# Hybrid decoder step on one core: the attention's output stores are issued by ScalarE instead of SP

## The chip, the cores and the metric

One NeuronCore of a Trainium2 chip runs the whole program in a single launch. The metric is device time in microseconds (us) of that launch. Engines are named as in the profile: PE is TensorE's matmuls and PEld its weight loads, DVE is VectorE, ACT is ScalarE, POOL is GpSimd, and SP is SyncE, which in this kernel issues nearly all DMAs. "SPq" and "ACTq" are the sequencers of those engines.

## The reference

One inference step of a decoder with a recurrent layer and an attention layer, for two groups of tokens:

```python
x = x + rms_norm(recurrent_mixer(rms_norm(x)))          # RG-LRU layer
k, v, logf = shared_kv(x)                               # K, V, log-forget, new rows
# attention layer, 16 heads of 64, queries q and gate g from x @ w_in:
s = q @ k^T * 64**-0.5 + cq[query] - ck[key]            # cq, ck: running sums of logf
s = where(k_pos <= q_pos, s, -inf)
o = softmax(s) @ v
x = x + rms_norm((o * silu(g)) @ w_out)
```

The first group is a new sequence ("prompt") of 2048 tokens of width 1024. The second is 8 sequences of 8 new tokens ("sample") that each attend over 4096 older keys and values, which lie in 32 pages of 128 rows each, found through a page table. All is float32; matmul operands are split into a high and a low part where that precision is wanted.

## The kernel before

The program goes through the recurrent layer in two chunks of tokens and through the projections to K, V, Q and the gate in three. Then comes the attention of the prompt, and last the output projection. The attention over the old pages ("decode") is a Python generator that is drawn on beside these: its work is dealt out into the projections and the prompt's attention by a table of costs. A scheduler of the framework then sets the final order on each engine from its own timeline; the two versions are scheduled separately, so instructions can change places well away from an edit.

**Prompt attention.** It consists of 64 *units*, one for each of 16 heads (`h`) and each quarter of 512 queries (`qc`). A unit goes through 4 to 16 key tiles of 128; over all units that is 640 ticks. Each tick is: a score tile `st` on PE (L1651 and L1652, and L1654 where the causal mask cuts), its exponential on ACT (L1662), a running sum on POOL (L111), and, two to eight ticks later in groups, the product with V on PE (`ops`, L1675). The score tiles have two PSUM banks while the decode runs. The maxima that the exponentials need come from a second pass of scores on PE (`sx`, L1438), which DVE reduces (L1440, L1444).

**The end of a unit.** `finish` (from L1465) books two steps with `later`, a list of functions due some ticks ahead. `copies` runs two ticks after the last product: ACT copies the unit's output from PSUM into a 64x512 tile `oT` (L1478, two copies; the profile calls that buffer `attw`, since it is a lent piece of one). `store` runs two ticks after that: SP writes `oT` to the DRAM tensor `og_d` (L1483; `ogd` in the profile). The buffers of `oT` serve four units in turn. `project` reads `og_d` back at the very end (L1732).

**Decode.** For each sequence and half of the heads ("turn"), SP loads 8 groups of four K pages (L1144) and 8 of four V pages (L1146) into four buffers `raw` of four pages each. DVE transposes the K pages (`ktr`, L1218), PE makes scores (`dS`, L1202), ACT exponentiates (L1256), PE multiplies with V pages straight from `raw` (`dO`, L1290).

**The order on SP.** SP takes its instructions strictly in order: page loads, loads of queries and keys (L1405 to L1421), stores. The helper `paged()` puts what is recorded inside it behind the newest page group on SP:

```python
    def paged():
        return tc.issue_after(place["S"]) if "S" in place else ExitStack()
```

**Completion semaphores.** The framework gives the DMAs that SP issues eight completion semaphores in turn (`DMAHW0` to `DMAHW7`). Each DMA first waits until the DMA before it on its semaphore has landed, so at most eight are under way, and the ninth waits for the first.

Of the kernel before, what the change touches and what calls it, by code (L numbers as in the profile page):

```python
# [28 lines left out]
HD = 64  # L29
# [61 lines left out]
def tile_hawk_fox(  # L91
# [8 lines left out]
    V, A, G, T, S = nc.vector, nc.scalar, nc.gpsimd, nc.tensor, nc.sync  # L100
# [19 lines left out]
    def paged():  # L120

        return tc.issue_after(place["S"]) if "S" in place else ExitStack()
# [49 lines left out]
    def dt_(name, shape):  # L172
        return dram.tile(shape, F32, name=name, tag=name)
# [6 lines left out]
    og_d = [dt_(f"ogd{qc}", [D, 512]) for qc in range(SEQ // 512)]  # L180
# [197 lines left out]
    later = Later()  # L378
# [985 lines left out]
    def attention(es):  # L1364
# [100 lines left out]
        def finish(u, ops, acc):  # L1465
            h, qc = units[u]
            pr, h2 = divmod(h, 2)
            if u % 8 == 0:
                oTs_["sums"] = rings["sums"]()
            sums = oTs_["sums"]  # L1470
            if u % 2 == 0:
                oTs_["o"] = rings["oT"]()
            oT = oTs_["o"][u % 2 * HD:(u % 2 + 1) * HD, :]

            def copies():
                view = oT.rearrange("d (a r c) -> d a r c", a=2, r=2)
                for r in range(2):
                    A.copy(view[:, :, r, :], ops[r * HD:(r + 1) * HD, :].rearrange("d (a c) -> d a c", a=2))  # L1478
                later.after(2, store)

            def store():
                with paged():
                    S.dma_start(og_d[qc][h * HD:(h + 1) * HD, :], oT)  # L1483

            later.after(2, copies)
            accs.append((qc, acc))
            if len(accs) == 4 or h == H - 1:
                later.after(2, lambda todo=accs[:]: total(h2, sums, todo, h >= H - 2))
                accs.clear()
            if u >= len(units) - 4:  # L1490
                later.after(5, lambda: norm(pr, sums, qc, 1))
            elif u % 8 == 7:
                later.after(5, lambda: norm(pr, sums, 0, 4))

        def total(h2, sums, todo, single):


            ps = maxima("tot")
            for qc, acc in todo:
                T.matmul(ps[qc * 32:(qc + 1) * 32, :], ones[:, :32], acc[:, :], start=True, stop=True)  # L1500
            cs = todo[-1][1]
            rows = slice(0, P) if len(todo) == 4 else slice(qc * 32, (qc + 1) * 32)
            A.copy(cs[rows, :], ps[rows, :])
            if single:
                for qc, acc in todo:
                    j = qc * 2 + h2
                    S.dma_start(sums[j * 16:(j + 1) * 16, :], cs[qc * 32:qc * 32 + 1, :].rearrange("o (r c) -> o r c", r=16))
            else:
                S.dma_start(sums[h2 * HD:(h2 + 1) * HD, :], cs[:, :].rearrange("(q z) (r c) -> z q r c", z=32, r=16)[0])

        def norm(pr, sums, q0, n):

            ps_ = slice(q0 * 32, (q0 + n) * 32)
            V.reciprocal(sums[ps_, :], sums[ps_, :])
            V.tensor_copy(rs[0][ps_, :], sums[ps_, :])
            tt(V, rs[1][ps_, :], sums[ps_, :], f(rs[0][ps_, :]), ALU.subtract)
            for x in range(2):
                if n == 4:
                    for z in range(2):
                        S.dma_start(r_d[:, x, z, pr, :].rearrange("q (r c) -> q r c", r=16),  # L1520
                                    f(rs[x][z * HD:(z + 1) * HD, :]))
                else:
                    S.dma_start(r_d[q0, x, :, pr, :].rearrange("z (r c) -> z r c", r=16), f(rs[x][ps_, :]))
# [119 lines left out]
        for u, (h, qc) in enumerate(units):  # L1643
            for k in range(nks[u]):
# [21 lines left out]
                def product(u=u, h=h, todo=pair, early=group == 8, acc=acc, last=(k == nks[u] - 1)):  # L1666


                    nonlocal ops
                    if todo[0][0] == 0:  # L1670
                        ops = ops2[:, u % 2 * 256:u % 2 * 256 + 256]

                    def mm(k, lo, p, r):
                        a0 = (lo // P + 1 - r) // 2
                        return T.matmul(ops[r * HD:(r + 1) * HD, a0 * P:], vvs[h % 2][:, k, :],  # L1675
                                        p[:, :].rearrange("p (a r c) -> p a r c", a=2, r=2)[:, a0:, r, :],
                                        start=(k == 0), stop=(last and k == todo[-1][0] - 1 + r))

                    together([partial(mm, k, lo, p, r) for k, lo, p, _ in todo for r in range(2) if lo <= (2 + r) * P],
                             [todo[-1][3]])  # L1680
                    for k, lo, p, _ in todo:
                        if k and not early:
                            tt(a_l(), acc[:, lo:], acc[:, lo:], p[:, lo:], ALU.add)
                    if last:
                        finish(u, ops, acc)
# [329 lines left out]
```

## Time and profile before

| | |
|---|---|
| time, 3 runs | 2919.55, 2931.59 (median), 2937.87 us |
| the profiled execution | 2919.81 us, span 2918.1 us |
| PE busy over the span | 2747.1 us (94%) |
| ACT busy over the span | 1267.6 us (43%) |
| granted PE clock | 0.978 of full speed |
| HBM traffic | 222 GB/s over the span |

The profile is of one execution. "Idle before, releaser" is time in which an engine stood still, and the instruction whose semaphore ended that. An engine's `DMA_DIRECT2D` row is the time that its sequencer takes to issue a DMA; the transfer itself runs on the 16 DMA engines afterwards.

### The profile page before, as it was taken

How to read it: one execution, taken by the hardware profiler on the slowest of the kernel's cores; microseconds unless marked ns; L12 is line 12 of the kernel's file. 1: busy time of each engine (PE TensorE's matmuls, PEld its weight loads, DVE VectorE, ACT ScalarE, POOL GpSimd, SP SyncE). 2: the span in 40 equal slices, each digit the busy share in tenths (PEclk: the TensorE clock that was granted, in tenths of full speed). 3: DMA queues.
4: the chain of work that ended last, by engine and by line, in shares of the span. 5: the costliest groups of instructions: out<-in, count | busy, mean ns of one | idle time of the engine just before them, and what ended most of it. 6: DMA issues, size and time to landing. Idle time of an engine off the chain costs nothing.

```text
span 2918.1 us, 59421 instructions
## 1 busy us (share of the span) xinstructions
PE 2747.1 (94%) x21086; PEld 2224.8 (76%) x21086; DVE 1828.1 (63%) x3971; ACT 1267.6 (43%) x2874; POOL 1098.0 (38%) x1207
## 2 busy tenths in 40 slices
PE   5998999999998999999999999999999999999998
PEld 5997789988898997887888766565666665666787
DVE  7877457244256775676565676767677766655465
ACT  4656342222234665533334345444444544455221
POOL 1654110000003652100001265756565655659554
PEclk9999999999999999999999999999999999999999
DMA  4224536789745536689999978778788777862454
GB/s 127 80 86 125 169 124 188 203 243 300 224 142 177 178 107 191 215 303 325 341 314 333 338 261 293 239 255 277 253 271 269 255 259 240 284 222 61 131 184 131
DMA packets 484789, 636.03 MB, mean 218 GB/s; under 512 B 100888, under 2 KB 293145, under 8 KB 477276
## 3 DMA queue, kind: packets, MB, share of 16 engines
q1 hardware_dynamic: 484204, 630.13, 66.6%
q8 instruction: 167, 2.74, 0.4%
q0 software_dynamic: 288, 2.10, 0.3%
q14 instruction: 130, 1.06, 0.1%
HBM read 512.78 MB, written 133.85 MB: 222 GB/s over the span
## 4 chain that ended last, share of the span: by engine, by line
PE 55%; DMA 9%; DVE 7%; ACT 4%; SPq 3%; issue 2%; POOL 1%; DVEq 0%; ACTq 0%; POOLq 0%
PE ops L1675 8%; PE st L1651 5%; PE sx L1438 4%; PE st L1652 4%; PE dS L1202 3%; PE dO L1290 3%; PE y L389 3%; PE y L387 3%; PE y L388 3%; DMA raw<-in_cache_k_dram 2%; PE kv L387 2%; PE kv L389 2%; PE kv L388 2%; PE qg L387 2%; PE qg L389 2%
## 5 line engine op out<-in xcount | busy, mean ns | idle before, releaser
L1218 DVE STREAM_TRANSPOSE ktr<-raw 128x1024 f32<-128x1024 f32 x256 | 308.0, 1225 | 97.6 <-DMA raw<-in_cache_k_dram 73.5
L1440 DVE TENSOR_REDUCE mxs<-sx 128x1 f32<-128x512 f32 x384 | 253.8, 680 | 157.6 <-PE sx L1438 156.8
L387 PE MATMUL kv<-wh,xh 128*128 128x256 f32 (+3 forms) x1088 | 307.7, 287 | 3.0 <-ACT wh L432 1.7
L389 PE MATMUL kv<-wh,xl 128*128 128x256 f32 (+3 forms) x1088 | 307.1, 284 | 0.4 <-DMA xl<-xld 0.4
L388 PE MATMUL kv<-wl,xh 128*128 128x256 f32 (+3 forms) x1088 | 306.6, 284 | 0.4 <-DVE wl L433 0.3
L433 DVE SCALAR_TENSOR_TENSOR wl<-wst,gv,wh 128x256 fp32r<-128x256 f32 (+1 forms) x384 | 171.1, 494 | 130.7 <-ACT wh L432 130.6
L432 ACT ACTIVATE wh<-wst,gv 128x256 fp32r<-128x256 f32 (+1 forms) x384 | 164.4, 499 | 200.4 <-DMA wst<-in_b_w_in_dram 83.0
L389 PE MATMUL qg<-xh,wl 128*128 128x384 f32 (+2 forms) x640 | 227.5, 357 | 2.2 <-DVE wl L433 2.2
L387 PE MATMUL qg<-xh,wh 128*128 128x512 f32 (+2 forms) x640 | 229.2, 359 | 0.0
L388 PE MATMUL qg<-xl,wh 128*128 128x512 f32 (+2 forms) x640 | 228.1, 358 | 0.0
L387 PEld LDWEIGHTS kv<-wh,xh 128*128 128x128 f32 (+1 forms) x1088 | 201.1, 186 | 8.7 <-issue 3.7
L389 PEld LDWEIGHTS kv<-wh,xl 128*128 128x128 f32 (+1 forms) x1088 | 202.3, 186 | 3.1 <-issue 2.4
L388 PEld LDWEIGHTS kv<-wl,xh 128*128 128x128 f32 (+1 forms) x1088 | 201.5, 186 | 4.1 <-issue 2.5
L1166 POOL TENSOR_TENSOR qw<-qb,amask 128x128 f32<-128x128 f32 x64 | 26.7, 422 | 459.9 <-PE dS L1202 197.7
L1662 ACT ACTIVATE attl<-st 128x512 f32<-128x512 f32 (+3 forms) x236 | 120.5, 524 | 129.2 <-PE st L1652 61.4
L1444 DVE CUSTOM_DVE_ANT_0 sx<-sx,maskb 128x128 f32<-128x128 f32 (+3 forms) x256 | 123.1, 488 | 70.9 <-PE sx L1438 64.9
L1662 ACT ACTIVATE attw<-st 128x512 f32<-128x512 f32 (+3 forms) x224 | 118.0, 550 | 102.4 <-PE st L1652 68.1
L1290 PE MATMUL dO<-raw,sc 128*32 128x256 f32 x2048 | 141.9, 398 | 20.7 <-DMA raw<-in_cache_v_dram 19.9
L111 POOL TENSOR_TENSOR atth<-atth,attl 128x512 f32<-128x512 f32 (+3 forms) x119 | 128.1, 1079 | 65.9 <-ACT attl L1662 47.7
L111 POOL TENSOR_TENSOR atth<-atth,attw 128x512 f32<-128x512 f32 (+3 forms) x116 | 132.3, 1141 | 38.9 <-ACT attw L1662 22.1
L1202 PE MATMUL dS<-ktr,qw 128*32 128x128 f32 x4096 | 129.8, 282 | 14.4 <-DVE ktr L1218 13.5
L925 ACT COPY kf<-kv 128x256 f32<-128x256 f32 (+1 forms) x136 | 49.0, 366 | 217.1 <-PE kv L389 152.7
(359 smaller groups left out, 7651.8 us busy)
## 6 DMA issues: line engine op xcount, KB each, us to landing
raw<-in_cache_k_dram SPq DMA_DIRECT2D x512, 256.0 KB
raw<-in_cache_v_dram SPq DMA_DIRECT2D x512, 256.0 KB
wst<-in_w_kv_dram SPq DMA_DIRECT2D x48, 512.0 KB
wst<-in_b_w_in_dram SPq DMA_DIRECT2D x48, 512.0 KB
xt<-in_x_prompt_dram SPq DMA_DIRECT2D x32, 512.0 KB
wst<-in_a_w_in_dram SPq DMA_DIRECT2D x64, 256.0 KB
out_dram<-kf SPq DMA_DIRECT2D x128, 128.0 KB
cb<-cd SPq DMA_DIRECT2D x14, 1024.0 KB
```

What stands on the lines that cost most here:

```text
L111: eng.tensor_tensor(out, a, b, op=op)
L387: T.matmul(ps, lh(k), rh(k), start=(k == 0), stop=False)
L388: T.matmul(ps, lh(k), rl(k), start=False, stop=False)
L389: end = T.matmul(ps, ll(k), rh(k), start=False, stop=(k == nk - 1))
L432: A.activation(wh[:, k, :], st[:, k, :], AF.Copy, scale=gk)
L433: V.scalar_tensor_tensor(wl[:, k, :], st[:, k, :], gk, f(wh[:, k, :]), op0=ALU.mult, op1=ALU.subtract)
L1202: return T.matmul(sp[c * 32:(c + 1) * 32, h * P:(h + 1) * P], qw[:, pp * 2 + h // 2, h % 2 * 2 + x, :], kt[:, :, :, i0:i0 + 8], start=(x = ...
L1218: behind("V", V.transpose(t.kts[pp][:, n], raw[:, :, pp * 256:(pp + 1) * 256]).ins)
L1290: return T.matmul(op[c:c + 32, :256], t.sc[:, i // 4, m, a * 4:(a + 1) * 4, :].rearrange("p h q -> p (h q)"), raw[:, m, a * 256:(a + 1) * ...
L1440: r = V.reduce_max(mx[:, j, ck:ck + 1], ps[:, :w], axis=AX.X)
L1662: pair.append((k, lo, p, A.activation(p[:, lo:], ps[:, lo:], AF.Exp)))
L1675: return T.matmul(ops[r * HD:(r + 1) * HD, a0 * P:], vvs[h % 2][:, k, :], p[:, :].rearrange("p (a r c) -> p a r c", a=2, r=2)[:, a0:, r, : ...
```

## The change

The function `store` goes. ACT issues the store itself, in `copies`, right behind its two copies:

```diff
                 for r in range(2):
                     A.copy(view[:, :, r, :], ops[r * HD:(r + 1) * HD, :].rearrange("d (a c) -> d a c", a=2))
-                later.after(2, store)
-
-            def store():
-                with paged():
-                    S.dma_start(og_d[qc][h * HD:(h + 1) * HD, :], oT)
+                A.dma_start(og_d[qc][h * HD:(h + 1) * HD, :], oT)
 
             later.after(2, copies)
```

64 DMAs of 128 KB move from SP's queue to ACT's. Lines behind the edit have numbers lower by four in the changed kernel (L1662 becomes L1658). Nothing else is written differently.

The first place is on SP, around the store of the second unit (`ogd_73`); the words in brackets are the semaphores that an instruction waits for: a DMA's own completion semaphore and those of engines. `TENSOR_LOAD` and `ISA` fetch page numbers. Before:

```order
L1144 DMA raw<-in_cache_k_dram 128x512 [waits DMAHW5_49]
L1421 DMA qa_17881<-qd 128x512 [waits DMAHW6_49]
L1415 DMA qbt_17880<-qd 64x512 [waits DMAHW7_49,PE_49]
L1483 DMA ogd_73<-attw 64x512 [waits DMAHW0_49,Activation_49]
L1136 TENSOR_LOAD pt_130
L1146 ISA
L1146 DMA raw<-in_cache_v_dram 32x4x512 [waits DMAHW1_49,PE_49]
```

and with the change:

```order
L1144 DMA raw<-in_cache_k_dram 128x512 [waits DMAHW5_49]
L1421 DMA qa_17881<-qd 128x512 [waits DMAHW6_49]
L1415 DMA qbt_17880<-qd 64x512 [waits DMAHW7_49,PE_49]
L1136 TENSOR_LOAD pt_130
L1146 ISA
L1146 DMA raw<-in_cache_v_dram 32x4x512 [waits DMAHW1_49,PE_49]
```

The store is gone from between the query load and the V page; the V page keeps its semaphore, number 1, and so number 0 is still passed over for the store.

The second place is on ACT, around the copies of the same unit. Before:

```order
L1478 COPY attw<-ops 64x2x128 [waits PE_49]
L1478 COPY attw<-ops 64x2x128
L1459 ACTIVATE qbt_17877<-mps,st_p 4x128 [waits PE_49,Pool_49]
L1459 ACTIVATE qbt_17877<-mps,st_p 4x128 x3
L1662 ACTIVATE atth_19402<-st 128x512 [waits PE_49,Pool_49]
```

and with the change:

```order
L1478 COPY attw<-ops 64x2x128 [waits PE_49]
L1478 COPY attw<-ops 64x2x128
L1459 ACTIVATE qbt_17877<-mps,st_p 4x128 [waits PE_49,Pool_49]
L1459 ACTIVATE qbt_17877<-mps,st_p 4x128 x3
L1479 DMA ogd_73<-attw 64x512 [waits DMAHW0_49,Activation_49]
L1658 ACTIVATE atth_19402<-st 128x512 [waits PE_49,Pool_49]
```

The store now stands on ACT ahead of the next exponential, and it brings both of its waits with it: for ACT's own copies, and for `DMAHW0`, whose DMA before it is one that SP issues.

## Prediction

> **What bounds the kernel now.** I read the page's head first, then the busy times by stage, then the waits of the stage in which the stores lie.
>
> ```profile
> span 2918.1 us, 59421 instructions
> core 0: us, PE busy (x) PEld busy (x) DVE busy (x) ACT busy (x) POOL busy (x), PEclk, DMA share, GB/s
> 0.00:1670.00 1670.00, 1563.40 (x11355) 1428.65 (x11355) 1012.51 (x2258) 724.50 (x1555) 347.93 (x519) 0.98 0.66 209
> 1670.00:2640.00 970.00, 916.75 (x8469) 593.72 (x8467) 659.54 (x1352) 461.95 (x1141) 590.86 (x568) 0.97 0.78 259
> 2640.00:2725.00 85.00, 82.71 (x476) 53.81 (x477) 36.02 (x83) 42.93 (x100) 68.31 (x62) 0.96 0.16 43
> ```
>
> The rows are stretches of the span. The prompt's attention runs from 1670 to about 2725 us, up to 2640 with the transfers busy (DMA share 0.78) and then without them (0.16). The stores lie there and nowhere else; up to the first of them the order on all engines is the same in both versions, so the first 1670 us stay. PE is busy 916.75 + 82.71 = 999.5 of 1055 us: it is the bound, and only its 55.5 idle us can be won. What PE waits for there:
>
> ```profile
> PE dO L1290 <- DMA raw<-in_cache_v_dram: 13.5, 6, 3.4
> PE sx L1438 <- DVE mxs L1440: 7.5, 13, 1.5
> PE st L1651 <- ACT attl L1662: 7.3, 16, 1.5
> PE sx L1438 <- DVE mxs L1444: 5.0, 4, 2.3
> PE st L1651 <- ACT attw L1662: 4.3, 12, 1.5
> PE dS L1202 <- DVE ktr L1218: 2.5, 1, 2.5
> PEld dO L1290 <- DMA raw<-in_cache_v_dram: 6.3, 8, 2.8
> ```
>
> Each row gives total us, times, longest. Late pages cost PE 13.5 us and its weight loads 6.3 (partly the same moments), late K transposes 2.5, late exponentials 7.3 + 4.3.
>
> **What the change takes from SP.**
>
> ```profile
> SPq L1483 <- ACT attw L1478: 55.9, 22, 7.5
> SPq L1483 <- ACT attw L1478: 37.4, 18, 5.5
> SPq L1483 <- ACT attw L1478: 18.5, 4, 7.5
> SPq L1146 <- DVE ktr L1218: 14.2, 4, 7.0
> SPq L1146 <- PE dO L1290: 12.8, 3, 6.9
> L1483 SPq DMA_DIRECT2D ogd<-attw x64: 463/521/1447, 1678.0 to 2722.3; - x64
> ```
>
> The first three rows are SP's wait at the store for ACT's copies: in the whole attention, before 2640, and after. 37.4 us of it hold up page loads. The last row gives the issue of one store (minimum, median, maximum): 64 x 0.521 = 33 us that also leave SP. How much of this reaches PE? Never more than late pages cost: 13.5 + 6.3 + 2.5 = 22.3 us, and the rows of L1146 say that a page load that comes earlier often meets a buffer that is still in use (14.2 + 12.8 us). Of PE's long waits for V pages, the loads just ahead show this:
>
> ```profile
> 1847.79 1.98 SPq L1144 DMA_DIRECT2D raw<-in_cache_k_dram  x4
> 1857.76 3.13 SPq L1146 DMA_DIRECT2D raw<-in_cache_v_dram  x4
> 1864.34 1.83 PE L1290 MATMUL dO<-raw,sc 128*32 128x256 f32 x16 [2.07 <-DMA raw<-in_cache_v_dram]
> 2339.02 0.54 SPq L1483 DMA_DIRECT2D ogd<-attw  x1
> 2339.75 0.60 SPq L1146 DMA_DIRECT2D raw<-in_cache_v_dram  x1
> ```
>
> At 1864 us the V pages were late because their loads stood still until 1857.76 behind no store. At 2339 a store stood in a burst of page loads and put the next one off by 2339.75 - 2339.02 = 0.73 us. I take one or two such slots, 0.7 to 1.4 us, for each of PE's six waits, 4 to 8 us, and put the gain at **5 us** (ends 0 and 22). The 18.5 us after 2640 I put at nothing: no page follows there, and PE is busy 82.71 of 85 us.
>
> **What it puts on ACT: the issue.** No DMA is issued by ACT in this trace. The nearest row is SP's 0.521 us above; the ends are nothing and 64 x 0.521 = 33 us. What covers it is ACT's own idle time in front of its exponentials:
>
> ```profile
>   PE st L1652: 181.6, 170
>   PE st L1654: 123.5, 114
>   PEld st L1651: 60.3, 141
>   PE st L1651: 14.1, 37
> ```
>
> Of 640 exponentials 170 + 114 = 284 begin after ACT waited for PE, 305.1 / 284 = 1.07 us each; the rest follow without a pause. The last two rows are the other side: 141 of PE's 640 score tiles already wait for an exponential, since with two banks tile k+2 needs the exponential of tile k. So 22% of delays on ACT hit PE at once (7 us of 33), and at most the 56% that meet no pause (18 us). I take **9 us**, near the lower, because that one is counted at PE itself.
>
> The Trainium skill ("Perfetto Trace Analysis", DMA Instruction — HWDGE) says that such an interval ends when the sequencer "is now free for the next instruction". By it ACT is blocked for the whole 0.52 us, as assumed; if the issue instead ran beside the next exponential, the term would be 0. No row here shows ACT issuing.
>
> **What it puts on ACT: a wait for SP's transfers.** This is the term that decides. The store must find its completion semaphore free, and the DMA before it there is one of SP's, eight issues earlier. SP, which comes by in its own order, finds that mostly over; ACT comes when its copies are done. The unit whose order was shown:
>
> ```profile
> 1689.30 0.59 SPq L1405 DMA_DIRECT2D atth<-kd  x1
> ...
> 1695.04 0.58 SPq L1415 DMA_DIRECT2D qbt<-qd  x1
> 1697.56 0.52 SPq L1483 DMA_DIRECT2D ogd<-attw  x1
> 1691.70 0.74 ACT L1478 COPY attw<-ops 64x256 f32<-64x256 f32 x2 [3.34 <-PE ops L1675]
> 1692.47 1.11 ACT L1459 ACTIVATE qbt<-mps,st_p 4x128 fp32r<-4x128 f32 x4
> 1694.33 0.60 ACT L1662 ACTIVATE atth<-st 128x512 f32<-128x512 f32 x1 [0.76 <-PE st L1652]
> 2720.38 0.74 ACT L1478 COPY attw<-ops 64x256 f32<-64x256 f32 x2
> 2722.25 0.58 SPq L1483 DMA_DIRECT2D ogd<-attw  x1
> ```
>
> The copies end at 1691.70 + 0.74 = 1692.44; the store goes out only at 1697.56, 5.1 us later, though SP had nothing to issue from 1695.62 on: the key load L1405 of 1689.30 (1 MB) is its predecessor on the semaphore. On ACT the store will be reached at 1692.47 + 1.11 = 1693.58 and keep the exponential of 1694.33 waiting until about 1697.5. Between that unit and the last one (2721.12 to 2722.25, 1.1 us) 35 of the 64 stores go out more than 0.25 us after their copies, 88 us in sum. 88 us is the upper end of ACT's wait, since in this execution every predecessor had landed by the time of the store, and 0 the lower, if SP pulls ahead enough.
>
> Where between? In a burst SP issues thus, and transfers take so long:
>
> ```profile
> 1967.39 3.55 SPq L1146 DMA_DIRECT2D raw<-in_cache_v_dram  x4
> 2339.75 5.91 DMA raw<-in_cache_v_dram
> 2508.61 3.03 DMA raw<-in_cache_v_dram
> ```
>
> Eight issues take 0.65 to 0.9 us each, 5 to 7 us; the transfers on the chain of waits take 3 to 6. At SP's own place the predecessor is done for some 1.1 us on average, so of each lateness I strike 1.1 us: 52 us are left, in 27 units. Half of the stores stand behind one more exponential (0.6 us), which takes 8 off: **44 us in about 19 waits**. Since SP no longer stops for ACT, it will run ahead of where it was; I strike a third, 29 us. ACT's pauses swallow up to 1 us of each wait, and what is left of the 29 is about 17: **17 us** of late score tiles on PE.
>
> **The sum.** -5 (pages) + 9 (issue) + 17 (waits) = +21. A PE that comes later finds other inputs ready: of its 13.5 + 7.5 + 5.0 + 2.5 = 28.5 us for pages and DVE I let a third, 9 us, go under. That leaves **+12 us**: 2919.8 + 12 = 2932 on the scale of the profiled execution, which ran 11.8 us under the median; on the median, 2931.6 + 12 = **2943 us**. The two schedules also differ in many small swaps on PE and DVE, which the trace can't price; they stand on either side.
>
> **The rivals.**
>
> *ACT's waits pass through whole* (ends slower). SP doesn't pull ahead: it is held by buffers (L1146 above), and each stop of ACT makes PE release those buffers later, so SP stays as late as now. ACT then waits near 88 us in 35 places, less 1 us of pause each is 53, plus 9 for issues, less 5 and 9: +48, **2980 us**. It decides from a mean wait of 2 us at the 64 stores. For it: the lateness is seen. Against it: in 22 units SP was early, and gains 37.4 us.
>
> *SP's freedom wins* (ends faster). SP's 37.4 us move every later page ahead, the predecessors land before ACT comes, and the issues sit in ACT's pauses. Then only the gain is left, 5 to 22 us: about -12, **2920 us**. For it: DMA share 0.78, so transfers have room. Against it: PE's waits for pages mostly follow other causes.
>
> *The change does little either way.* The two waits cancel and only SP's issue time is saved, which lies beside PE's work: -4 to +4, **2931 us**. The Trainium skill ("DMA: Bandwidth & Descriptors", Issuing engines are not separate DMA queues) states this case: all issuers share the 16 DMA engines, and issuing from several "will only save the time on the sequencer". The trace agrees that SP has 33 us of such time; the rule leaves out that the new issuer can stop.
>
> **How the numbers follow.** My forecast 0.43, waits passing whole 0.22, SP's freedom 0.20, little either way 0.15. The range takes in the forecast, the gain down to its end (2931.6 - 22 = 2910) and the rival's time with half its spread: 2908 to 2982; left out are 0.10 above and 0.07 below. A measurement of this kernel tells about 1% (29 us) from no change. Faster by more needs more than every page wait gone: 0.08. Slower by more is the first rival and a tail of the forecast: 0.25. Within: 0.67.
>
> **What would show it.** Right: waits of ACT at L1479 or behind it for DMAs, 20 to 45 us in 15 to 25 places; waits of PE for exponentials grown from 14 to some 30 us; no wait of SP for L1478; waits for V pages a little under 13.5; attention (first store to last) 5 to 25 us longer. Wrong: if ACT's waits are under 10 us, SP did pull ahead; if the store's issue on ACT is far from 0.52 us, that term goes; if stages before 1670 us differ, it is not this change.

## The result, and the profile after

| | before | after |
|---|---|---|
| time, 5 runs each (median, lowest to highest) | 2928.39 us (2919.55 to 2937.87) | 2954.63 us (2948.39 to 2956.55) |
| the profiled execution | 2919.81 us, span 2918.1 us | 2951.92 us, span 2950.2 us |
| granted PE clock of the profiled execution | 0.978 | 0.973 |

The changed kernel takes 1.0105 times as long, with a 95% interval of 1.0082 to 1.0128: 26 us more by the medians. The forecast was 12 us more. A second measurement, told below, gave 1.0095 (1.006 to 1.013).

The stages of the changed kernel, as the first rows of the prediction show them for the kernel before (stretch in us, its length, then the busy time of each engine, the granted PE clock, the DMA share and GB/s):

```profile
span 2950.2 us, 59327 instructions
core 0: us, PE busy (x) PEld busy (x) DVE busy (x) ACT busy (x) POOL busy (x), PEclk, DMA share, GB/s
0.00:1670.00 1670.00, 1560.28 (x11352) 1423.47 (x11353) 1010.50 (x2256) 724.36 (x1555) 348.70 (x520) 0.99 0.66 209
1670.00:2640.00 970.00, 900.15 (x8272) 578.34 (x8272) 633.24 (x1316) 439.73 (x1098) 563.61 (x547) 0.95 0.76 251
2640.00:2757.00 117.00, 111.91 (x679) 72.17 (x676) 62.55 (x126) 65.01 (x143) 93.75 (x82) 0.98 0.33 102
```

Up to 1670 us nothing moved. The first exponential of the attention ends at 1670.6 us before and at 1670.7 us after, the stretch behind the last one takes 213.0 and 213.1 us. From the first to the last of the 640 exponentials it is 1034.5 us before and 1066.5 us after: all 32 us of the profiled pair are in the attention, and "in the attention" below means from the first to the last of these exponentials. Two numbers of the second row against the row of before carry the rest. PE is busy 900 us of 970 instead of 917, and its granted clock there is 0.95 instead of 0.97.

PE's waits by what ended them (total us, times, longest), of after:

```profile
PE dO L1290 <- DMA raw<-in_cache_v_dram: 16.6, 7, 7.2
PE st L1647 <- ACT attl L1658: 12.5, 17, 3.8
PE st L1647 <- ACT atth L1658: 10.8, 10, 4.3
PE sx L1438 <- DVE mxs L1440: 9.4, 14, 1.5
PE st L1647 <- ACT attw L1658: 6.8, 15, 2.7
PE sx L1438 <- DVE mxs L1444: 3.6, 5, 1.7
PE sx L1438 <- ACT qbt L1459: 3.3, 2, 3.1
```

and who waits for the exponentials, now L1658, in all (us, times):

```profile
  PEld st L1647: 71.2, 132
  PE st L1647: 30.1, 42
```

PE waits 30.1 us for exponentials where it waited 14.1, and 16.6 us for V pages where it waited 13.5. What holds up ACT are DMAs that SP issued:

```profile
ACT attw L1658 <- DMA qbt<-qd: 6.8, 1, 6.8
ACT qbt L1459 <- DMA raw<-in_cache_k_dram: 6.1, 1, 6.1
ACT attl L1658 <- DMA raw<-in_cache_v_dram: 5.3, 2, 3.9
ACT atth L1658 <- DMA raw<-in_cache_v_dram: 5.3, 1, 5.3
ACT atth L1658 <- DMA atth<-kd: 4.1, 1, 4.1
ACT atth L1658 <- DMA raw<-in_cache_k_dram: 2.0, 1, 2.0
ACT attl L1658 <- DMA raw<-in_cache_k_dram: 1.9, 1, 1.9
ACT attl L1658 <- DMA qbt<-qd: 0.9, 1, 0.9
```

These are 32.4 us in 9 waits, and in each of the nine places the instruction ahead on ACT is a store. The exponential itself reads `st`, which none of these rows names: it is late because the store ahead of it stood for its completion semaphore. The trace shows that directly. The 64 stores use the same eight semaphores as SP's DMAs, and each of these nine stores is issued 0.08 us behind the last update of its semaphore by a DMA of SP's. One of the nine in order of time (start, duration, engine, line, operation, in brackets the idle time ahead of it and what ended that):

```profile
1903.87 1.95 PE L1202 MATMUL dS<-ktr,qw 128*32 128x128 f32 x64
1903.98 0.75 ACT L1478 COPY attw<-ops 64x256 f32<-64x256 f32 x2 [4.62 <-PE ops L1671]
1907.75 1.07 PE L1290 MATMUL dO<-raw,sc 128*32 128x256 f32 x16 [0.49 <-DMA raw<-in_cache_v_dram]
1910.28 0.45 ACTq L1479 DMA_DIRECT2D ogd<-attw  x1
1910.78 1.10 ACT L1459 ACTIVATE qbt<-mps,st_p 4x128 fp32r<-4x128 f32 x4 [6.06 <-DMA raw<-in_cache_k_dram]
1911.94 0.44 PE L1438 MATMUL sx<-atth,attl 96*128 96x384 f32 x1 [3.12 <-ACT qbt L1459]
1913.23 3.56 PE L1202 MATMUL dS<-ktr,qw 128*32 128x128 f32 x64
```

ACT's copies end at 1904.73, the store goes out at 1910.28, 5.55 us later, when a K page has landed. ACT stands for 6.06 us and PE for 3.12 us. And the 64 score matmuls of the decode, which took 1.95 us ahead of the stop, take 3.56 us behind it. The stretches around it say why:

```profile
1895.00:1906.00 11.00, 10.40 (x134) 7.21 (x133) 6.66 (x16) 4.03 (x9) 6.34 (x8) 1.00 0.90 309
1906.00:1913.00 7.00, 3.21 (x26) 1.72 (x25) 3.36 (x8) 2.19 (x6) 0.75 (x2) 1.00 0.76 246
1913.00:1917.00 4.00, 4.00 (x67) 3.19 (x66) 0.32 (x3) 0.60 (x1) 3.86 (x5) 0.57 0.83 263
```

After the gap PE is granted 0.57 of its clock for 4 us (3.4 us at a half, the rest full). So a stop is paid twice: as idle time, and as a few us of slow matmuls in which PE counts as busy. Summed over the trace's records of the clock, 14 stretches at half the clock begin between 1670 and 2725 us before, 61.4 us long, and 19 between 1670 and 2757 us after, 99.0 us long. Half of that length is lost, 30.7 and 49.5 us, but only where PE works: of the half-clock time in the attention 3.1 us before and 13.8 us after lie in gaps, where it costs nothing more. So the two parts are best read at PE itself. Its idle time in the attention is 53.6 us before and 71.7 us after, 18.1 us more; its busy time, for the same work, is 980.9 and 994.8 us, 13.9 us more. Together they are the 32.0 us. The records of the clock give nearly the same for the second part: the half-clock time outside the gaps grows from 61.1 to 85.4 us, and half of that is 12 us.

### The profile page after: what moved, and what is told of

Same layout as the page of the kernel before. It is cut to its first block, busy times and chain, and to the rows that moved or that the text cites. A ratio compares the mean times of both kernels' runs of the same rounds, so it can differ in the third digit from the quotient of the medians.

```text
span 2950.2 us, 59327 instructions
## 1 busy us (share of the span) xinstructions
PE 2756.7 (93%) x21086; PEld 2222.8 (75%) x21086; DVE 1825.3 (62%) x3971; ACT 1266.7 (43%) x2874; POOL 1096.4 (37%) x1207
## 4 chain that ended last, share of the span: by engine, by line
PE 61%; DMA 12%; DVE 10%; ACT 6%; SPq 6%; issue 3%; POOL 1%; ACTq 0%; DVEq 0%; POOLq 0%
PE ops L1671 7%; PE st L1647 4%; PE y L389 4%; PE y L387 4%; PE y L388 4%; PE sx L1438 4%; PE st L1648 3%; PE dO L1290 3%; PE dS L1202 3%; DMA raw<-in_cache_k_dram 3%; PE kv L389 3%; PE kv L387 3%; PE kv L388 3%; PE qg L389 2%; PE qg L387 2%
## 5 line engine op out<-in xcount | busy, mean ns | idle before, releaser
L1658 ACT ACTIVATE attl<-st 128x512 f32<-128x512 f32 (+3 forms) x236 | 121.1, 524 | 131.3 <-PE st L1648 58.2
L1658 ACT ACTIVATE attw<-st 128x512 f32<-128x512 f32 (+3 forms) x224 | 117.7, 549 | 114.0 <-PE st L1648 69.4
L111 POOL TENSOR_TENSOR atth<-atth,attl 128x512 f32<-128x512 f32 (+3 forms) x119 | 127.9, 1078 | 78.3 <-ACT attl L1658 55.9
L1658 ACT ACTIVATE atth<-st 128x512 f32<-128x512 f32 (+3 forms) x180 | 92.7, 522 | 108.4 <-PE st L1650 47.5
```

The source lines that it names most:

```text
L111: eng.tensor_tensor(out, a, b, op=op)
L1658: pair.append((k, lo, p, A.activation(p[:, lo:], ps[:, lo:], AF.Exp)))
```

## The experiments

Three theories were on record. **A**: ACT stops at completion semaphores that it shares with SP's loads, PE stops with it and runs on at half the clock. **B**: the time to issue 64 DMAs on ACT is what costs. **C**: the scheduler's different order, or the place of the store in the code, is what costs. Each kernel was timed in 5 rounds against the kernel before on the same chip.

**ACT as busy as the issues make it, without a DMA** (B against A):

```diff
 # kernel before; SP still issues the stores
                     A.copy(view[:, :, r, :], ...)
+                A.copy(oT[:, :336], oT[:, :336])
```

> SP issues the stores as before; instead of the DMA, ACT copies 64x336 of the finished unit onto itself right behind its two copies, about 0.45 us, waiting for its own copies as the store did, but for no transfer. Theory A (ACT stops at the completion semaphores that it shares with SP, and PE stops with it and then runs some us at half clock): 0 to 8 us over the kernel before, waits of PE for exponentials near 74 us (PE and weight loads together). Theory B (the 0.45 us on ACT in front of the exponentials, 64 times, is the cost): 20 to 30 us over the kernel before. Theory C (it is the other order that the scheduler makes): within 8 us of the kernel before, either side.

Measured: 1.0015 (0.9995 to 1.0034), some 4 us. The row of the added copies (us in all, ns of one):

```profile
L1479 ACT COPY attw<-attw 64x336 f32<-64x336 f32 x64 | 30.0, 468 | 1.5
```

30 us more work on ACT raise PE's idle time from 53.6 to 57.8 us and leave its half-clock time at 61.4 us. B falls: 64 issues of 0.45 us cannot explain 26 us.

**Two stores for each unit, on ACT** (the waits of A made more):

```diff
-                A.dma_start(og_d[qc][h * HD:(h + 1) * HD, :], oT)
+                for z in range(2):
+                    A.dma_start(og_d[qc][h * HD + z * 32:h * HD + z * 32 + 32, :], oT[z * 32:z * 32 + 32, :])
```

> The changed kernel with each store issued as two of 64 KB, 128 DMAs on ACT. Theory A: the second half waits for the next semaphore, whose transfer of SP was issued one place later, so ACT's waits grow from 31 to 40-60 us and the time is 36 to 45 us over the kernel before. Theory B: 64 more issues of 0.45 us, 50 us or more over the kernel before, with the waits for transfers unchanged. Theory C: within 8 us of the changed kernel.

Measured: 1.0138 (1.0116 to 1.0161), some 40 us over the kernel before. Counted at the stores themselves (those issued more than 0.25 us after ACT was free for them), ACT's waits are 53 us in 27 places, where the changed kernel has 31 us in 11. And who waits for the exponentials:

```profile
  PEld st L1648: 77.5, 108
  PE st L1648: 44.2, 39
```

PE's idle time is 82.5 us, and 112.6 us are at half the clock. Cost and waits grow together, as A has it.

**SP's store booked 8 ticks behind the copies instead of 2** (what SP's freedom is worth without ACT):

```diff
-                later.after(2, store)
+                later.after(8, store)
```

> The kernel before with the store on SP booked 8 ticks behind the copies instead of 2. SP then never waits for ACT's copies (55.9 us before), and ACT issues nothing. If SP's waits at the stores were worth what the prediction gave them, 5 us: 0 to 8 us under the kernel before. If they were worth nothing: within 4 us. If SP's place in the order is what matters (theory C), it may differ by more, either side.

Measured: 0.9997 (0.998 to 1.0013). It did not do what it was made for. SP still waits for the copies:

```profile
SPq L1483 <- ACT attw L1478: 42.8, 19, 6.6
```

that is 42.8 us instead of 55.9: the store still stands on SP ahead of the time when its data is ready, so the later booking hardly moved it. So this run says little on SP's freedom; the next one does.

**GpSimd issues the stores** (neither SP nor ACT):

```diff
-                A.dma_start(og_d[qc][h * HD:(h + 1) * HD, :], oT)
+                G.dma_start(og_d[qc][h * HD:(h + 1) * HD, :], oT)
```

> The store issued by GpSimd in the place where the changed kernel has ACT issue it. GpSimd's DMAs have completion semaphores of their own, so neither ACT nor GpSimd waits for SP's transfers. Theory A and theory B: ACT free again, within 8 us of the kernel before, unless the issue on GpSimd (unknown, perhaps 1 us each, 64 us on an engine that is busy 60%) delays the running sums. Theory C (SP without the stores, another order): near the changed kernel, 20 us or more over.

Measured: 1.0012 (0.9998 to 1.0025). POOL's stores have completion semaphores of their own, and now the wait for the copies is POOL's; the row of its waits is

```profile
POOL ogd L1479 <- ACT attw L1478: 98.3, 37, 6.5
```

and who waits for the exponentials:

```profile
  PE st L1647: 11.8, 35
```

No wait of ACT for a DMA is left at the stores, PE waits 11.8 us for exponentials, its idle time is 55.4 us and its half-clock time 64.9 us, all near the kernel before. Two things follow. The code is the changed kernel's but for the engine, so the place of the store in the code is not the cause. And SP, freed of all 64 stores, gains nothing: PE's waits for V pages are 14.8 us here against 13.5.

**SP issues the store at the place where the change puts it** (C once more):

```diff
-                A.dma_start(og_d[qc][h * HD:(h + 1) * HD, :], oT)
+                S.dma_start(og_d[qc][h * HD:(h + 1) * HD, :], oT)
```

> The store stands in the code where the change puts it, right behind the copies and without being put behind the newest page, but SP issues it as before. Theory A: no wait on ACT, so the kernel before within 0.4%; SP still waits some 30 to 60 us for the copies, which PE does not see. Theory C (the place in the code and the order that the scheduler makes of it): as with the change, +20 us or more.

Measured: 0.9994 (0.998 to 1.0009). SP waits 54.8 us for the copies at the store and PE doesn't notice. With this run, C falls as far as it means the place.

As far as C means the order on PE, the last two runs say little, for they keep nearly the order of the kernel before. A line-by-line difference of PE's order in the traces, with equal neighbours taken as one of 12397 rows, has 722 lines (those gone and those new) for the changed kernel, 99 with GpSimd and 15 here. But the kernel with 64 short copies has 670 such lines and costs 4 us, and a kernel told below has 7 and costs 23. So another order alone does not explain the loss, and the loss comes without another order.

**The same sum of ACT time in long pieces.** Is a stop of ACT enough, without any DMA? In three kernels ACT copies bytes onto themselves, each piece in one instruction:

```diff
 # kernel before, behind the copies; 14 units x 1.89 us
+                if u % 9 in (1, 5):
+                    A.copy(oT.bitcast(mybir.dt.uint8), oT.bitcast(mybir.dt.uint8))
 # second kernel: 28 units x 1.04 us
+                if u % 9 in (1, 3, 5, 7):
+                    A.copy(oT[:, :256].bitcast(mybir.dt.uint8), oT[:, :256].bitcast(mybir.dt.uint8))
 # third kernel: 8 units x 3.60 us
+                if u % 8 == 5:
+                    pair = wide12[8][HD:, :1024].bitcast(mybir.dt.uint8)
+                    A.copy(pair, pair)
```

> The kernel before, SP still issues the stores; after the copies of 14 of the 64 units ACT also copies the tile onto itself as 2048 single bytes, one instruction of some 2.2 us by its element count (14 x 2.2 = 31 us, as much ACT time as the 64 short copies of the earlier run, and as much as ACT's 31 us of waits with the change, in about as many pieces). No DMA is touched. Theory A (a stop of ACT stops PE, and PE runs on at half the clock): each piece makes a gap of 1 to 2 us on PE, together 14 to 24 us more idle time, 4 to 6 more stretches at half the clock (30 to 45 us, half of it lost), +28 us in all (22 to 40). The same without the clock (theory A as predicted, the term missing): +14 to 24 us with the half-clock time as before (about 61 us). Theory B or C (the issue, or the order): 0 to 8 us.

> As the run with 14 pieces, but 28 pieces of half the size (1.2 us each, 33 us in all). If the length of the single stop decides: ACT's pauses of about 1.07 us swallow most of each piece, the gaps on PE stay under 1 us and leave the clock alone: 4 to 12 us more idle time, half-clock time within 10 us of before, +5 to 15 us. If the sum of ACT's time decides: the same as with 14 pieces, +22 to 40 us.

> The kernel before with one byte copy of 4096 elements (about 3.7 us by the 1.89 us of the 2048-element one) on ACT in 8 of the 64 units, 30 us in all: the same sum of ACT time as 28 x 1.04 and 14 x 1.89 us, in fewer and longer pieces, as long as the longer waits with the change. Theory A with the clock: gaps of some 2.6 us on PE, 8 x 2.6 = 21 us more idle time, and nearly every one followed by 3.4 or 6.8 us at half the clock, 14 to 20 us lost beyond that: +35 us (26 to 44). Without a clock term that grows with the length of the stop: +16 to 22 us, half-clock time within 10 us of before.

Measured: 14 pieces (26.5 us) 1.0049 (1.0028 to 1.007); 28 pieces (29.1 us) 1.0039 (1.0022 to 1.0056); 8 pieces (28.8 us) 1.0013 (0.9993 to 1.0033). This went against A as it was put: the longest pieces cost least, +4 us where 26 to 44 were expected, the 14 pieces cost 14 us where 22 to 40 were, and half-clock time stayed at 54.6 to 71.7 us in all three. The time of the 28 pieces came out as expected, for a reason that the third kernel puts in doubt. Its order of time shows why the test did not make the stop that was meant:

```profile
2343.33 3.60 ACT L1481 COPY attw<-attw 64x4096 uint8<-64x4096 uint8 x1
2343.46 0.41 PE L1654 MATMUL st<-attl,atth 128*128 128x512 f32 x1
2343.70 0.40 PE L1655 MATMUL st<-qbt,atth 128*128 128x512 f32 x1
2345.07 0.49 PE L1438 MATMUL sx<-kbt,qbt 96*128 96x512 f32 x1 [0.17 <-DVE mxs L1440]
2346.79 0.83 PE L1438 MATMUL sx<-kbt,qbt 96*128 96x512 f32 x2 [1.23 <-DVE mxs L1440]
```

and who waits for its exponentials:

```profile
  PE st L1654: 13.7, 28
```

While ACT copies, PE works on score tiles for the maxima (`sx`), which need no exponential, and its waits for exponentials stay at 13.7 us. Over the eight copies, each taken to 1.5 us behind its end, PE is idle 10.9 us in all, of 28.8 us of copying. The scheduler can plan such a copy and orders PE's work around it: by the count above PE's order differs in 1066 lines from the kernel before. A stop that the order provides for is here nearly free. The wait at a store's semaphore depends on when a transfer lands, so what was wanted is a stop that the scheduler does not know of.

**A stop that the order does not provide for.** A square root needs another function table on ACT than the exponentials; both loads are put in behind the scheduler:

```diff
 # kernel before, behind the copies; 11 units (second kernel: u % 3 == 1, 21 units)
+                if u % 6 == 1:
+                    z = small.tile([P, 1], F32, name="ss", tag="ss")
+                    A.activation(z[:HD, :], oT[:, :1], AF.Sqrt, scale=0.0)
```

> The kernel before; behind the copies of 11 of the 64 units ACT also takes the square root of one column, scaled to zero, into a spare tile. That needs another function table: two loads of 1.28 us each (the row of such loads in the profile before) and the small instruction, some 2.8 us in one stop, 31 us in all, which the scheduler does not see when it orders PE (the order on PE differs from before in 9 rows, while with the 8 long pieces it differs in 1039 and score tiles for the maxima stand beside the pieces). No DMA is touched. Theory A with the clock (a stop that the order did not provide for opens a gap on PE, and PE then runs at half the clock): PE's idle time +15 to 22 us, half-clock time +25 to 45 us (half of it lost), +26 to 40 us in all, as with the change. If the loss needs the stores on ACT's queue itself or the other order: +0 to 6 us, as with the 8 long pieces. If only the gaps count and not the clock: +15 to 22 us.

> As the run with 11 square roots, with 21 of them: 59 us of stops that the order does not provide for, near the 52 to 55 us of waits with two stores for each unit (which cost 40 us). Theory A with the clock: PE's idle time +30 to 40 us, half-clock time +45 to 80 us, +45 to 75 us in all. Without the clock: +30 to 40 us. If the stores themselves are what costs: 0 to 8 us.

Measured: 1.0086 (1.006 to 1.0111) with 11, 1.0144 (1.012 to 1.0167) with 21: +23 and +45 us by the medians, with no DMA touched and the stores on SP. One stop of the first in order of time:

```profile
2328.68 0.76 ACT L1478 COPY attw<-ops 64x256 f32<-64x256 f32 x2 [2.84 <-PE ops L1678]
2329.46 1.28 ACT L1481 ACT_TABLE_LOAD   x1
2330.75 0.20 ACT L1481 ACTIVATE ss<-attw 64x1 f32<-64x1 f32 x1
2330.97 1.28 ACT L1665 ACT_TABLE_LOAD   x1
2332.26 0.60 ACT L1665 ACTIVATE attl<-st 128x512 f32<-128x512 f32 x1
2332.91 0.80 PE L1654 MATMUL st<-attl,atth 128*128 128x512 f32 x1 [2.67 <-ACT attl L1665]
```

and who waits for its exponentials:

```profile
  PEld st L1654: 80.8, 146
  PE st L1654: 32.3, 44
```

11 stops of 2.78 us (2.80 from 2329.46 to 2332.26), 31 us in all, do to PE what the change does: 32.3 us of waits for exponentials in 44 places against 30.1 in 42, and 70.8 us of idle time against 71.7. The row at 2332.91 also has the slow clock: a score matmul of 0.80 us where 0.40 is usual. With 21 stops PE waits 45.6 us and idles 88.5 us. Over the 11 stops, each again taken to 1.5 us behind its end, PE is idle 19.4 us, against 10.9 us over the eight longer copies. That ACT stands where PE's order did not expect it is therefore enough; the DMA in it is only the means. One difference between these kernels was not separated: the copies and the table loads stand in different units.

On the clock this pair says less than was expected. The profiled execution with 11 stops has 61.4 us at half the clock, no more than before, and it was also the quickest of its six runs (2937.5 us, the others 2941.2 to 2958.6). Over all six the mean granted clock is 0.9760 against 0.9779 for the kernel before beside them, about 6 us (2926 x 0.0019 / 0.976). With 21 stops it is 0.9746, about 10 us of the 45, so there too the idle time came out as expected (+35 us) and the clock's part smaller.

**The changed kernel once more**, for a second profile:

> The changed kernel once more, beside the one with the 8 long pieces, for a second profile: +22 to 32 us; if the terms found are real and not of one execution, PE's idle time in the attention is again 15 to 22 us over the kernel before, and the half-clock time 25 to 45 us over it.

Measured: 1.0095 (1.006 to 1.013), +28 us by the means. PE's idle time in the attention is 73.0 us and its half-clock time 105.8 us, its waits for exponentials 29.5 us: the terms of the first profile hold. The mean granted clock over the six runs is 0.9733, over the 17 of the kernel before 0.9786: 2923 x 0.0053 / 0.9733 = 16 us.

What stays open is why the same idle time brought 16 us of slow clock with the change and 6 us with the table loads. The lengths differ: the profile after has seven gaps of 3.0 us or more on PE from 1670 to 2757 us (one before, none with 11 table loads), and in all seven half the clock begins inside the gap or within 1.3 us behind it. The longest, 7.2 us, is a wait for V pages and not for an exponential. Longer stops that the scheduler doesn't know of were not tried on their own.

## Why the prediction was right or wrong, by its own steps

**Right: what bounds the kernel, and that ACT's wait decides.** The first 1670 us and the tail stayed. ACT's waits for SP's transfers were put at 29 us and are 32.4 us by the rows of waits. PE's waits for exponentials were to grow from 14 to some 30 us and are 30.1. SP waits for L1478 no longer. From the first store to the last it is 1044.3 us before and 1074.2 us after, 29.9 us more, over the 5 to 25 us that were named as a sign.

**Wrong in shape: "about 19 waits".** There are 9, and they are longer, 3.6 us each instead of 1.5. For the idle time that made little difference; longer gaps are the ones that the clock follows.

**The step that failed: the sum counted a stop only as idle time.** The sum of the four terms, +12, has no term for the clock. The rows of before had one to read: 0.97 in the attention, 14 stretches at half the clock, most of them just behind a gap on PE. That term is 14 us in the profiled pair (32.0 less 18.1 of idle time) and 16 us over the runs, more than the whole forecast. The rest of the sum came nearer, 18.1 us of idle time for +12, and in part by luck: two savings that did not come, 5 and 9 us, stand against 9 us for the issue that is at most 4. The Trainium skill (TensorE: Matmul & The Clock Gate, HAM oscillation — how this bites in real kernels) states the rule as "no PE-idle gaps >~3.4µs". Of the gaps of 2.0 to 2.9 us in the run with 11 table loads, 10 of 12 were already followed by 3.4 or 6.8 us at half the clock, so here the measurement puts the danger lower than the rule.

**The absorption, -9, failed.** "A third of PE's 28.5 us of waits for pages and DVE" was to go under in its lateness. The V pages went up from 13.5 to 16.6 us, the waits for DVE's maxima from 12.5 to 13.0. One thing that works against the absorption can be seen: SP's loads of queries wait longer for buffers that PE must free first, first the two rows of before, then of after:

```profile
SPq L1421 <- PE st L1654: 20.6, 5, 8.7
SPq L1415 <- PE st L1652: 18.7, 11, 9.4
SPq L1415 <- PE st L1648: 38.6, 15, 13.6
SPq L1421 <- PE st L1650: 32.8, 7, 8.4
```

That these waits are what made the V pages late is not shown.

**The pages, -5, failed.** SP was freed of 55.9 us of waits and PE gained none of it; with the stores on GpSimd, where ACT is not disturbed, it gained none either. The lower end that was given, 0, is right.

**The issue, +9, was too much.** The issue takes 0.453 us, near the 0.52 us assumed, but half of the time it stands beside an exponential. The row of the stores' issue (minimum, median, maximum in ns):

```profile
L1479 ACTq DMA_DIRECT2D ogd<-attw x64: 452/453/491, 1677.5 to 2751.7; - x64
```

and one of them in order of time:

```profile
2550.43 0.60 ACT L1658 ACTIVATE attw<-st 128x512 f32<-128x512 f32 x1
2550.46 0.45 ACTq L1479 DMA_DIRECT2D ogd<-attw  x1
2551.01 0.60 ACT L1658 ACTIVATE attw<-st 128x512 f32<-128x512 f32 x1
```

The store is issued at 2550.46 inside the exponential that started at 2550.43, and the next follows without a pause. In 33 of the 64 stores the issue starts inside an instruction that is already running on ACT, and in 17 of these the next one follows without a pause. As much real work on ACT costs 4 us (the run with 64 short copies), so the issue costs about that at most. The count that the 9 us lean on, 141 of 640, was also read too high: those are waits of PE's weight loads, which overlap with its matmuls, and PE's own row beside it has 37, or 6%. Taken with the waits, ACT's lateness was put at 9 + 17 = 26 us on PE; PE's own rows give 16.0 for the exponentials and, on that scale, little for the row of maxima that ACT writes into the queries (L1459, 3.3 us after).

**The rivals.** That the waits pass through whole has the right sign and comes out too high: 32 us and not 88. Of its reasons one is borne out, SP does stay held by buffers (the rows above). (The 22 units named against it are the waits that make up 55.9 us; the 37.4 us belong to 18.) That SP's freedom wins is refuted by the run with GpSimd. That little changes either way fails for the reason given with it: the new issuer can stop. With GpSimd as the issuer, where nothing that PE needs stops, it is what happened.

## What to carry to other kernels

Before a DMA is moved to an engine that computes, ask which completion semaphore it will wait for and who issues the DMA ahead of it there: a computing engine that stands behind another queue's transfer stops everything that feeds on it. Price a stop of a PE-bound stage at its idle time and add the slow clock behind it, which was here 16 us beside 18 us of idle time (the change) and 6 us beside 17 (11 table loads). And a stop that the order knows of can be filled: 8 copies of 3.6 us that the scheduler saw cost 4 us, 11 stops of 2.8 us that it didn't see cost 23.

## What was not expected of the hardware

- Half the clock followed most gaps on PE of 2 to 3 us (10 of 12 with 11 table loads), in pieces of 3.4, 6.8 or 10.2 us; 64 equal matmuls took 1.95 us ahead of a gap and 3.56 us behind it.
- ACT's queue issues a DMA while the exponential ahead of it still runs (33 of 64 times beside a running instruction); the 0.453 us are then at least partly hidden. Issued by GpSimd a store takes 0.546 us, by SP 0.521 us.
- The executions of one kernel spread with the granted clock: over 77 runs of the kernel before, the time falls by 2.3 us for each 0.001 of it (correlation -0.75).
